# Feed-forward GEMMs of a decoder trunk in groups of two column blocks, six of sixteen k tiles by seven block products instead of eight

## The chip, the cores and the metric

One NeuronCore of a Trainium2 chip runs the whole program in one launch. The metric is the device time of that launch in microseconds. The other engines beside TensorE (PE) are VectorE (DVE), ScalarE (ACT), GpSimd (POOL) and SyncE (SP), which issues nearly all DMAs.

## The reference, cut to what matters

A two-layer decoder trunk on 256 tokens of width 2048, all in float32. Each layer is attention, an output projection, and a SwiGLU feed-forward of inner width 5632; layer a has sparse attention, layer b dilated attention, and both also attend to 256 memory tokens. What the change rewrites is the feed-forward:

```python
def swiglu(h, w_gate, w_up, w_down):
    return (jax.nn.silu(h @ w_gate) * (h @ w_up)) @ w_down
...
    h = h + o
    return h + swiglu(rms_norm(h, norm_ffn), w_gate, w_up, w_down)
```

`w_gate` and `w_up` are 2048 x 5632, `w_down` is 5632 x 2048. The output is the last `h` after a final RMSNorm.

## The kernel before

Float32 accuracy comes from splitting. Every operand is written as hi + lo (two numbers of PE's float32r type): `split` lets ACT copy the source into `hi` (L56) and DVE subtract it, giving `lo` (L57); with a gain the lines are L59 and L60. One product of a 128 x 128 tile of x (stationary) by a 128 x 512 tile of weights (moving) is `mm3`, three matmuls: hi by hi (L64), and the two mixed ones (L65, L66).

A GEMM makes 256 tokens by 512 columns: two PSUM banks (one per token half `tt`), k in 128-row tiles. `load_w` brings weights by DMA in chunks of two k tiles (128 x 1024, 512 KB) into `raw` (four buffers), then splits the chunk into `whi` and `wlo` (three buffers each). `Gemm.run` then issues four `mm3` per chunk. The pools `wp` and `mm_ps` are opened once at the top and live through the whole program; the transposition tiles `aux` have three, later four PSUM banks.

In the feed-forward (`ffn`) each of 11 blocks of 512 columns does a gate GEMM, Silu on ACT (L744), an up GEMM, and a product on DVE (L750) that gives the tile `hb`. Four PE transposes per token half (`heads_T`, L231) turn `hb` into k tiles for the down GEMM, evicted from `aux` by ACT (`hThi`) and DVE (`hTlo`). The transposes are deferred: `at(..., 2, 4)` lists them as side steps, and `Side.tick` runs one after so many `mm3` of the next GEMM. The blocks are done in two halves, six and five, each followed by four down GEMMs of 24 or 20 k tiles whose sums are added to the residual `h`.

What sets the order: PE runs strictly in the order in which the program is written. The other queues (DVE, ACT, SP, POOL) are put in order by a scheduler at build time, and each then runs in that fixed order, waiting by semaphores.

Before the first FFN stands `project_out("a_w_out", ...)`, between the layers a GEMM on `w_kv_shared`, and before the second FFN `project_out("b_w_out", ...)`.

Of the kernel before, what the change touches and what calls it, by code (L numbers as in the profile page):

```python
# [8 lines left out]
F32 = mybir.dt.float32  # L9
# [7 lines left out]
P = 128  # L17
# [8 lines left out]
NFA = 6  # L26
# [5 lines left out]
CK = 2  # L32
# [3 lines left out]
def decoder_trunk(ctx: ExitStack, tc: tile.TileContext, a: dict, out: bass.AP):  # L36
# [3 lines left out]
    wp = ctx.enter_context(tc.tile_pool(name="wp", bufs=4))  # L40
    xp = ctx.enter_context(tc.tile_pool(name="xp", bufs=4))
# [66 lines left out]
    class Gemm:  # L108
        def __init__(self, chunks, xs, ncols, nk, gain=None):
            self.chunks, self.xs, self.ncols, self.nk, self.gain = chunks, xs, ncols, nk, gain  # L110
            self.k = 0
            self.ps = [mm_tile() for _ in range(2)]
# [47 lines left out]
    cs = const.tile([P, 2, 2, HD], F32, name="cs")  # L160
    gains = const.tile([P, 7, KT], F32, name="gains")
    mask_a = const.tile([P, 2 * P], BF16, name="mask_a")
    mask_c = const.tile([P, 2, NCMP], BF16, name="mask_c")
    peT = const.tile([P, 2, 32], F32, name="peT")
    gbias = const.tile([P, 36], F32, name="gbias")
    w2 = const.tile([P, 2, 2, HD], F32, name="w2")
    h = const.tile([P, 2, D], F32, name="h")
    const.tile([P, 80], F32, name="padc")
# [38 lines left out]
    def new_xs():  # L207
        ts = [pair(lambda i: xp.tile([P, 4, T], F32R, tag=("xhi", "xlo")[i], name=("xhi", "xlo")[i]))
              for _ in range(4)]
        xs = [(t[0][:, i, :], t[1][:, i, :]) for t in ts for i in range(4)]  # L210
        return ts, xs

    def residual_block(ps, nb, ssq, ts, gain=None):
# [4 lines left out]
        deferred.extend(at([lambda k2=k2: to_xT(nb, k2, ts, gain) for k2 in range(2)], 3, 5))  # L218

    def to_xT(nb, k2, ts, gain):  # L220
        srcs = [h[:, tt, (nb * 4 + k2 * 2 + i) * P:(nb * 4 + k2 * 2 + i + 1) * P]
                for i in range(2) for tt in range(2)]
        dst = tuple(t[:, k2 * 2:k2 * 2 + 2, :].rearrange("p c t -> p (c t)") for t in ts[nb])
# [13 lines left out]
    def scaled_tables(r, scale, tag):  # L237
        t = small.tile([P, 2, 2, HD], F32, tag=tag, name=tag, bufs=1)
# [123 lines left out]
    def load_memT(c):  # L362
        if c > 0:
# [4 lines left out]
            memT.extend((t[0][:, i, :], t[1][:, i, :]) for i in range(2))  # L368
# [4 lines left out]
    def load_first(i):  # L373
# [4 lines left out]
        memT.append((first_t[0][:, i, :], first_t[1][:, i, :]))  # L378
# [62 lines left out]
    mem_v(ps, mv_b)  # L441
    tab_k = scaled_tables(x_r, 1.0, "tabk")
# [4 lines left out]
    KTt = [pair(lambda i: pa.tile([P, 2, 272], F32R, name=f"KT{g}{i}")) for g in range(2)]  # L447
    V = [pair(lambda i: pa.tile([P, 2, 256], F32R, name=f"V{b}{i}")) for b in range(2)]
# [252 lines left out]
    def project_out(name, nk, ready, gi):  # L701
        ts, xs = new_xs()
        ssq = new_ssq()
        gain = lambda k: gains[:, gi, k:k + 1]
# [8 lines left out]
        for i in range(2):  # L713
# [3 lines left out]
            residual_block(g[i].ps, i, ssq, ts, gain)  # L717
        for nb in range(2, 4):
            ps = gemm(ob[nb], osx, 512, nk)
            residual_block(ps, nb, ssq, ts, gain)  # L720
        return xs, finish_rstd(ssq, 4)

    xs, f_r = project_out("a_w_out", KT, 6, 2)
    sub.close()
    stack.close()

    def ffn(pre, xs, f_r, fp, down_last):
        gb = wblocks(pre + "_w_gate", NFB, KT // CK)
        ub = wblocks(pre + "_w_up", NFB, KT // CK)

        def half(b0, b1):
            hs = []

            def to_hT(hb):
                t = pair(lambda i: fp.tile([P, 4, T], F32R, tag=("hThi", "hTlo")[i], name=("hThi", "hTlo")[i], bufs=7))
                hs.extend((t[0][:, i, :], t[1][:, i, :]) for i in range(4))
                return heads_T(hb, t)

            for b in range(b0, b1):
                ps = gemm(gb[b], xs, 512, KT)  # L740
                sg = []
                for tt in range(2):
                    s = fp.tile([P, 512], F32, tag="sg", name="sg", bufs=2)
                    nc.scalar.activation(s, ps[tt], AF.Silu, scale=f_r[:, tt:tt + 1])  # L744
                    sg.append(s)
                ps = gemm(ub[b], xs, 512, KT)
                hb = []
                for tt in range(2):
                    t = work.tile([P, 512], F32, tag="hb", name="hb", bufs=4)
                    nc.vector.scalar_tensor_tensor(t, ps[tt], f_r[:, tt:tt + 1], sg[tt], op0=ALU.mult, op1=ALU.mult)  # L750
                    hb.append(t)
                deferred.extend(at(to_hT(hb), 2, 4))
            return hs

        hs = half(0, NFA)
        w = a[pre + "_w_down0"]
        for nb in range(4):
            ps = gemm([w[nb, c] for c in range(4 * NFA // CK)], hs, 512, 4 * NFA)
            for tt in range(2):
                hbk = h[:, tt, nb * 512:(nb + 1) * 512]  # L760
                nc.vector.tensor_add(hbk, ps[tt], hbk)
        hs = half(NFA, NFB)
        w = a[pre + "_w_down1"]
        n = 4 * (NFB - NFA)
        down_last([[w[nb, c] for c in range(n // CK)] for nb in range(4)], hs, n)

    with tc.tile_pool(name="fa", bufs=1) as fp:
        def down_last(db, hs, n):
            global_ssq = new_ssq()
            ts, nxt = new_xs()  # L770
            for nb in range(4):
                ps = gemm(db[nb], hs, 512, n)
                residual_block(ps, nb, global_ssq, ts)
# [242 lines left out]
```

## Time and profile before

| | |
|---|---|
| three timed runs | 2092.44, 2093.40, 2094.06 us (median 2093.4) |
| the profiled execution | 2094.15 us, its span 2092.4 us |
| PE busy | 2077.3 us, 99% of the span, 9687 matmuls in the records |
| DVE, ACT busy | 1203.0 us (57%), 1009.5 us (48%) |
| first matmul of feed-forward a | 417.28 us |
| the two stretches shown below | 438.5 to 1127 us in feed-forward a, 1372.6 to 2072 us in feed-forward b |
| DMA | 396 MB, 189 GB/s over the span |

A PE row's duration includes the pipeline's fill and drain, so the pace of PE is the distance between the starts of matmuls, not their duration. The same holds a little for DVE and ACT: of two instructions that stand back to back the second starts some 0.08 us before the first has ended.

### The profile page before, as it was taken

Reading aid. Unit: us, or ns where it says so; the run is one execution under the profiler, and the core shown is the slowest. Engines: PE = TensorE matmul, PEld = TensorE weight load, DVE = VectorE, ACT = ScalarE, POOL = GpSimd, SP = SyncE. Lnnn points to the kernel's source line nnn. Section 1 sums busy time; section 2 is a strip of 40 time slices with the busy share of each in tenths; the row PEclk is TensorE's granted clock in tenths of the full one; section 3 lists DMA queues with packets and bytes.
Section 4 is the critical chain, followed back from the end, with each engine's and each line's share of the span. In section 5 each row is a group of like instructions: output and inputs, shape, how many; then the busy total and the mean of one; then the engine's idle time right before and its main releaser. Section 6 shows DMA issues by size and latency. Waiting matters only on the chain.

```text
span 2092.4 us, 25692 instructions
## 1 busy us (share of the span) xinstructions
PE 2077.3 (99%) x9687; PEld 1726.9 (83%) x9687; DVE 1203.0 (57%) x1727; ACT 1009.5 (48%) x1384; POOL 7.0 (0%) x26
## 2 busy tenths in 40 slices
PE   9999999999999999999999999999999999999998
PEld 7898888888888888888888888888888888888886
DVE  6767897554444554445555678754445544445454
ACT  7655565544444433444444555644444434444443
POOL 0000000000000000000000000000000000000000
PEclk9999999999999999999999999999999999999999
DMA  8757634555555566555555654555555566655564
GB/s 302 240 183 242 210 101 142 183 189 191 190 188 189 189 194 195 190 188 190 188 191 184 196 168 142 183 190 188 189 190 190 190 193 193 189 191 190 189 193 152
DMA packets 112013, 396.31 MB, mean 189 GB/s; under 512 B 12944, under 2 KB 13328, under 8 KB 111504
## 3 DMA queue, kind: packets, MB, share of 16 engines
q1 hardware_dynamic: 111600, 393.61, 57.9%
q8 instruction: 76, 1.25, 0.3%
q10 hardware_dynamic: 288, 1.05, 0.1%
q14 instruction: 49, 0.40, 0.1%
HBM read 392.51 MB, written 2.10 MB: 189 GB/s over the span
## 4 chain that ended last, share of the span: by engine, by line
PE 97%; DVE 2%; ACT 1%; issue 0%; DMA 0%; SPq 0%; POOLq 0%; POOL 0%; DVEq 0%; ACTq 0%
PE mm L64 31%; PE mm L66 30%; PE mm L65 30%; PE aux L231 1%; PE aux L199 1%; PE aux L66 1%; PE aux L65 1%; PE aux L64 1%; DVE wlo L57 0%; PE cmp L514 0%; PE cmp L513 0%; DVE E L269 0%; DMA memT_raw<-in_memT_dram 0%; DVE E L641 0%; ACT whi L56 0%
## 5 line engine op out<-in xcount | busy, mean ns | idle before, releaser
L57 DVE TENSOR_TENSOR wlo<-raw,whi 128x1024 fp32r<-128x1024 f32 (+1 forms) x656 | 795.3, 1213 | 781.2 <-ACT whi L56 776.0
L56 ACT ACTIVATE whi<-raw 128x1024 fp32r<-128x1024 f32 (+1 forms) x656 | 690.6, 1053 | 891.9 <-PE mm L65 871.2
L64 PE MATMUL mm<-whi,xhi 128*128 128x512 f32 (+1 forms) x1856 | 724.6, 390 | 0.0
L66 PE MATMUL mm<-wlo,xhi 128*128 128x512 f32 (+1 forms) x1856 | 716.9, 386 | 0.0
L65 PE MATMUL mm<-whi,xlo 128*128 128x512 f32 (+1 forms) x1856 | 716.2, 386 | 0.0
L66 PEld LDWEIGHTS mm<-wlo,xhi 128*128 128x128 f32 x1856 | 348.4, 188 | 71.8
L65 PEld LDWEIGHTS mm<-whi,xlo 128*128 128x128 f32 x1856 | 348.9, 188 | 65.7
L64 PEld LDWEIGHTS mm<-whi,xhi 128*128 128x128 f32 x1856 | 348.6, 188 | 65.8
L64 PE MATMUL mm<-whi,hThi 128*128 128x512 f32 x704 | 275.2, 391 | 0.0
L66 PE MATMUL mm<-wlo,hThi 128*128 128x512 f32 x704 | 274.0, 389 | 0.0
L65 PE MATMUL mm<-whi,hTlo 128*128 128x512 f32 x704 | 273.9, 389 | 0.0
L66 PEld LDWEIGHTS mm<-wlo,hThi 128*128 128x128 f32 x704 | 132.1, 188 | 27.8
L65 PEld LDWEIGHTS mm<-whi,hTlo 128*128 128x128 f32 x704 | 132.2, 188 | 27.2
L64 PEld LDWEIGHTS mm<-whi,hThi 128*128 128x128 f32 x704 | 132.2, 188 | 26.8
L60 DVE SCALAR_TENSOR_TENSOR wlo<-raw,gains,whi 128x512 fp32r<-128x512 f32 x160 | 113.9, 748 | 46.4 <-ACT whi L59 46.1
L59 ACT ACTIVATE whi<-raw,gains 128x512 fp32r<-128x512 f32 x160 | 108.0, 718 | 60.9 <-PE mm L65 54.1
L64 PE MATMUL mm<-whi,ohi 128*128 128x512 f32 x256 | 102.1, 399 | 2.2 <-ACT whi L59 2.2
L66 PE MATMUL mm<-wlo,ohi 128*128 128x512 f32 x256 | 100.4, 392 | 0.1
L65 PE MATMUL mm<-whi,olo 128*128 128x512 f32 x256 | 100.2, 391 | 0.0
L64 PEld LDWEIGHTS mm<-whi,ohi 128*128 128x128 f32 x256 | 48.5, 189 | 12.3 <-ACT whi L59 3.2
L66 PEld LDWEIGHTS mm<-wlo,ohi 128*128 128x128 f32 x256 | 48.3, 189 | 11.0 <-DVE wlo L60 0.8
L65 PEld LDWEIGHTS mm<-whi,olo 128*128 128x128 f32 x256 | 48.6, 190 | 9.3
(235 smaller groups left out, 1104.7 us busy)
## 6 DMA issues: line engine op xcount, KB each, us to landing
raw<-in_a_w_gate_dram SPq DMA_DIRECT2D x88, 512.0 KB, 4.3
raw<-in_a_w_up_dram SPq DMA_DIRECT2D x88, 512.0 KB, 3.7
raw<-in_a_w_down_dram SPq DMA_DIRECT2D x88, 512.0 KB, 3.8
raw<-in_b_w_gate_dram SPq DMA_DIRECT2D x88, 512.0 KB, 4.1
raw<-in_b_w_up_dram SPq DMA_DIRECT2D x88, 512.0 KB, 3.8
raw<-in_b_w_down_dram SPq DMA_DIRECT2D x88, 512.0 KB, 4.3
raw<-in_a_w_out_dram SPq DMA_DIRECT2D x32, 512.0 KB, 3.8
raw<-in_b_w_in_dram SPq DMA_DIRECT2D x32, 512.0 KB, 4.1
```

The source lines that it names most:

```text
L56: nc.scalar.activation(hi, src, AF.Copy)
L57: nc.vector.tensor_sub(lo, src, hi.bitcast(F32))
L59: nc.scalar.activation(hi, src, AF.Copy, scale=gain)
L60: nc.vector.scalar_tensor_tensor(lo, src, gain, hi.bitcast(F32), op0=ALU.mult, op1=ALU.subtract)
L64: nc.tensor.matmul(o, l[0], r[0], start=start, stop=False)
L65: nc.tensor.matmul(o, l[1], r[0], start=False, stop=False)
L66: nc.tensor.matmul(o, l[0], r[1], start=False, stop=stop)
L199: nc.tensor.transpose(ps[:, i * P:(i + 1) * P], s, ident)
L231: nc.tensor.transpose(ps[:, i * P:(i + 1) * P], tok[tt][:, i * P:(i + 1) * P], ident)
```

## The change

The 11 gate and 11 up blocks become 11 groups: group b holds gate block b and up block b, so that a step works on two column blocks by two token halves, four banks `b1` to `b4`. For six of the sixteen k tiles of a group (three pairs, `NPR` = 3) the 2 x 2 block product (two k tiles by two token halves on the left, two k tiles by two column blocks on the right) is made by seven products of sums of blocks (Strassen's scheme) and not eight. The other ten k tiles are "plain" steps of four `mm3`. Group 0 of a layer is all plain (16 steps). The down GEMMs become groups too: the inner width is now done in three portions of 4, 4 and 3 blocks, and each portion has two down groups of 1024 columns over 16, 16 or 12 k tiles; the last portion of layer b keeps plain GEMMs. In all 30 groups have the seven products.

The sums on the token side are made once for each operand (`Paired.finish`, four extra 128-column tiles per pair) and split with it. Those on the weight side are made by DVE on 128 x 1536 "quarters" that a DMA of 768 KB brings (`q11`, `q12`, `q22`, `q21`), and each of the seven operands is split by ACT and DVE (`qhi`, `qlo`, two buffers). Some products serve two banks: ACT copies a bank (`keep`), DVE adds to or subtracts from banks and makes `rest`. `run_groups` interleaves the plain steps of a group with the seven products of the next, by a table (`spacing`).

Room is made for this: `whi`/`wlo` have two buffers in the FFN and not three, `aux` has one PSUM bank there and not four, and the pools are opened and closed by phase (attention a, FFN a, attention b, FFN b); the memory keys and values of layer b are written to DRAM early and read back.

The core of the diff (rewritten layout helpers, constants moved between pools and tables left out):

```diff
-NFA = 6
+PORTIONS = ((0, 4), (4, 8), (8, 11))
+NPR = 3
+NSL = 8
+QW = NPR * 512
...
-    wp = ctx.enter_context(tc.tile_pool(name="wp", bufs=4))
-    mm_ps = ctx.enter_context(tc.tile_pool(name="mm_ps", bufs=4, space=PSUM))
+    def open_phase(name, raws, parts, mms, auxs):
+        nonlocal wp, wbufs, mm_ps, mm_tags, aux_ps
+        wp = phase.enter_context(tc.tile_pool(name="w" + name, bufs=1))
+        wbufs = raws, parts
+        mm_ps = phase.enter_context(tc.tile_pool(name="m" + name, bufs=1, space=PSUM))
+        mm_tags = mms
+        phase.enter_context(aux_stack)
+        aux_ps = aux_stack.enter_context(tc.tile_pool(name="x" + name, bufs=auxs, space=PSUM))
+    ATT = (("mm", 4), ("mm", 4))
+    FFN = (("b1", 2), ("b2", 2), ("b3", 2), ("b4", 1))
...
+        def finish(self, q, f):
+            n = 4
+            if self.sums:
+                n = NSL
+                nc.vector.tensor_sub(f[:, 4, :], f[:, 0, :], f[:, 3, :])
+                nc.vector.tensor_sub(f[:, 6, :], f[:, 1, :], f[:, 0, :])
+                nc.vector.tensor_sub(f[:, 5, :], f[:, 4, :], f[:, 1, :])
+                nc.vector.tensor_add(f[:, 7, :], f[:, 2, :], f[:, 5, :])
+            split(self.S[0][:, q, :n, :], self.S[1][:, q, :n, :], f[:, :n, :])
...
+        def product(self, b, s, t, side, start=False):
+            hl = [fq.tile([P, QW], F32R, tag=n, name=n, bufs=2) for n in ("qhi", "qlo")]
+            split(hl[0], hl[1], t)
+            for q in range(NPR):
+                mm3(self.bank[b], self.op.slot(q, s), tuple(v[:, q * 512:(q + 1) * 512] for v in hl),
+                    start and q == 0, q == NPR - 1, True)
+                side.tick()
...
+            def s1():
+                self.q12 = self.load(1)
+                nc.vector.tensor_add(self.q11, self.q11, self.q12)
+                self.new(2)
+                self.product(2, 4, self.q11, side, True)
+                self.p5 = self.keep(2)
+            def s2():
+                self.q22 = self.load(2)
+                nc.vector.tensor_add(self.q11, self.q11, self.q22)
+                b2 = self.new(1)
+                self.product(1, 5, self.q11, side, True)
+                nc.vector.tensor_add(b2, b2, self.p1)
+                u2 = self.keep(1)
+                nc.vector.tensor_sub(self.bank[2], self.bank[2], u2)
+            def s3():
+                nc.vector.tensor_add(self.q12, self.q12, self.q22)
+                self.product(1, 6, self.q12, side)
+                self.r = fq.tile([P, 512], F32, tag="rest", name="rest", bufs=2)
+                nc.vector.tensor_sub(self.r, self.p5, self.bank[1])
...
+        def plain(self, c, side):
+            if c == 0:
+                self.new(3)
+            ws = load_w(self.rest[c], 512)
+            last = c == len(self.rest) - 1
+            k = self.k0 + c
+            for b in ((3, 0, 1, 2) if last else (0, 1, 2, 3)):
+                x = self.op.xs[k](b % 2)
+                mm3(self.bank[b], x, ws[b // 2], c == 0 and (b == 3 or self.k0 == 0), last, True)
+                side.tick()
+
+    def spacing(n):
+        base = {16: (3, 2, 2, 2, 2, 2, 2), 10: (2, 1, 1, 2, 1, 2, 1), 6: (1, 1, 1, 1, 0, 1, 1)}[n]
+        return base, n - sum(base)
...
-                deferred.extend(at(to_hT(hb), 2, 4))
+                deferred.extend(at(hop().heads(j, hb), 5, 8))
...
+    def open_ffn(name):
+        nonlocal fh, fq, fpool
+        fbufs[0] = 2
+        open_phase(name, 4, 2, FFN, 1)
...
+    phase.close()
+    open_phase("b", 4, 3, ATT, 4)
...
+    for i in range(4):
+        nc.gpsimd.dma_start(mb[i], memkv[i])
```

Two places in the queues, as the built programs have them.

SP where the output projection of layer a gives way to the FFN, before (names carry buffer numbers; in brackets the semaphores that a row waits for):

```order
L76 DMA raw_4360<-in_a_w_out_dram 128x1024 [waits DMAHW4_49,DVE_49]
L76 DMA raw_4378<-in_a_w_out_dram 128x1024 [waits DMAHW5_49,DVE_49]
L76 DMA raw_4396<-in_a_w_out_dram 128x1024 [waits DMAHW6_49,DVE_49]
L76 DMA raw_4432<-in_a_w_gate_dram 128x1024 [waits DMAHW7_49,DVE_49]
L76 DMA raw_4459<-in_a_w_gate_dram 128x1024 [waits DMAHW0_49,DVE_49]
L76 DMA raw_4486<-in_a_w_gate_dram 128x1024 [waits DMAHW1_49,DVE_49]
L76 DMA raw_4504<-in_a_w_gate_dram 128x1024 [waits DMAHW2_49,DVE_49]
```

The same place of SP now (`gu_0` holds the first gate and up blocks, `gu_q` the quarters):

```order
L98 DMA raw_4370<-in_a_w_out_dram 128x1024 [waits DMAHW0_49,DVE_49]
L98 DMA raw_4388<-in_a_w_out_dram 128x1024 [waits DMAHW1_49,DVE_49]
L98 DMA raw_4406<-in_a_w_out_dram 128x1024 [waits DMAHW2_49,DVE_49]
L98 DMA raw_4461<-in_a_gu_0_dram 128x1024 [waits DMAHW4_49,DMAHW5_49,DMAHW3_49,DMAHW6_49,DVE_49,PE_49]
L98 DMA raw_4488<-in_a_gu_0_dram 128x1024
L98 DMA raw_4515<-in_a_gu_0_dram 128x1024
L860 DMA q11_4533<-in_a_gu_q_dram 128x1536 [waits Pool_49]
L98 DMA raw_4551<-in_a_gu_0_dram 128x1024
L98 DMA raw_4569<-in_a_gu_0_dram 128x1024 [waits DMAHW7_49,DVE_49]
```

The first weights of the FFN waited for DVE's last read of one `raw` buffer; they now wait for PE too, and the count of that semaphore is the one which the last matmul of the output projection brings. The first weights of phase b and of FFN b wait in the same way.

DVE after a gate/up block, where the two token halves of `hb` are transposed (`hTlo<-aux` empties a transposition tile), before:

```order
L57 TENSOR_TENSOR wlo_6367<-raw_6364,whi_6366 128x1024
L750 SCALAR_TENSOR_TENSOR hb_6324<-mm_6178,rstd_4423,sg_6174 128x512
L750 SCALAR_TENSOR_TENSOR hb_6326<-mm_6179,rstd_4423,sg_6176 128x512
L57 TENSOR_TENSOR wlo_6385<-raw_6382,whi_6384 128x1024
L57 TENSOR_TENSOR hTlo_6329<-aux_6344,hThi_6328 128x4x128
L57 TENSOR_TENSOR wlo_6403<-raw_6400,whi_6402 128x1024
L57 TENSOR_TENSOR hTlo_6329<-aux_6357,hThi_6328 128x4x128
```

The same place of DVE now, after the fourth group of layer a:

```order
L78 TENSOR_TENSOR qlo_5924<-q11_5920,qhi_5923 128x1536
L983 SCALAR_TENSOR_TENSOR hb_5850<-mm_5322,rstd_4433,hb_5850 128x512
L983 SCALAR_TENSOR_TENSOR hb_5853<-rest_5427,rstd_4433,hb_5853 128x512
L78 TENSOR_TENSOR wlo_5891<-raw_5888,whi_5890 128x1024
L885 TENSOR_TENSOR q11_5920<-q11_5920,q12_5956 128x1536
L900 TENSOR_TENSOR q12_5956<-q12_5956,q22_5993 128x1536
L78 TENSOR_TENSOR wlo_5941<-raw_5938,whi_5940 128x1024
L78 TENSOR_TENSOR qlo_5961<-q11_5920,qhi_5960 128x1536
L78 TENSOR_TENSOR hTlo_4877<-aux_5897,hThi_4876 128x4x128
L78 TENSOR_TENSOR wlo_5978<-raw_5975,whi_5977 128x1024
L892 TENSOR_TENSOR q11_5920<-q11_5920,q22_5993 128x1536
L78 TENSOR_TENSOR hTlo_4877<-aux_5913,hThi_4876 128x4x128
```

One `wlo` stood between the second `hb` and the emptying of the first tile; now two `wlo`, two additions of quarters and a `qlo` stand there. With one `aux` bank PE's second four transposes (`aux_5913`) wait for that `hTlo`.

## Rows read from the trace of the kernel before

**Rows 1.** The page: busy time, share of span, instructions of each engine.

```profile
PE 2077.3 (99%) x9687; PEld 1726.9 (83%) x9687; DVE 1203.0 (57%) x1727; ACT 1009.5 (48%) x1384; POOL 7.0 (0%) x26
```

**Rows 2.** The page: chain that ended last, by engine.

```profile
PE 97%; DVE 2%; ACT 1%; issue 0%; DMA 0%; SPq 0%; POOLq 0%; POOL 0%; DVEq 0%; ACTq 0%
```

**Rows 3.** Windows over both feed-forwards: length, busy us per engine, clock, DMA, GB/s.

```profile
438.50:1127.00 688.50, 688.50 (x3093) 570.09 (x3092) 346.77 (x313) 297.91 (x311) 0.00 (x0) 1.00 0.59 190
1372.60:2072.00 699.40, 699.40 (x3129) 579.12 (x3128) 353.14 (x321) 299.99 (x310) 0.00 (x0) 1.00 0.59 190
```

**Rows 4.** Timeline of a gate GEMM: start, duration, engine, line, op, tiles.

```profile
599.38 1.23 DVE L57 TENSOR_TENSOR wlo<-raw,whi 128x1024 fp32r<-128x1024 f32 x1 [0.93 <-ACT whi L56]
...
600.53 0.68 DVE L57 TENSOR_TENSOR hTlo<-aux,hThi 128x512 fp32r<-128x512 f32 x1
...
601.53 0.39 PE L64 MATMUL mm<-whi,xhi 128*128 128x512 f32 x1
...
604.22 1.06 ACT L56 ACTIVATE whi<-raw 128x1024 fp32r<-128x1024 f32 x1 [1.66 <-PE mm L65]
...
604.25 0.39 PE L64 MATMUL mm<-whi,xhi 128*128 128x512 f32 x1
```

**Rows 5.** Groups by line and shape: count, busy us, mean ns, idle before.

```profile
L57 DVE TENSOR_TENSOR wlo<-raw,whi 128x1024 fp32r<-128x1024 f32 x640 | 783.7, 1225 | 769.5 <-ACT whi L56 764.4 <-PE cmp L514 2.0
...
L56 ACT ACTIVATE whi<-raw 128x1024 fp32r<-128x1024 f32 x640 | 680.0, 1063 | 877.8 <-PE mm L65 858.2 <-issue 8.0 <-PE cmp L513 3.4
...
L750 DVE SCALAR_TENSOR_TENSOR hb<-mm,rstd,sg 128x512 f32<-128x512 f32 x44 | 32.2, 748 | 0.0
L57 DVE TENSOR_TENSOR hTlo<-aux,hThi 128x512 fp32r<-128x512 f32 x44 | 30.3, 688 | 7.4 <-ACT hThi L56 7.4
...
L56 ACT ACTIVATE hThi<-aux 128x512 fp32r<-128x512 f32 x44 | 26.0, 590 | 21.1 <-PE aux L231 21.1
...
L60 DVE SCALAR_TENSOR_TENSOR xlo<-aux,gains,xhi 128x256 fp32r<-128x256 f32 x32 | 14.6, 480 | 4.2 <-ACT xhi L59 4.1
L59 ACT ACTIVATE xhi<-aux,gains 128x256 fp32r<-128x256 f32 x32 | 14.3, 466 | 1.8 <-PE aux L199 1.8
...
L57 DVE TENSOR_TENSOR wlo<-raw,whi 128x548 fp32r<-128x548 f32 x16 | 11.6, 726 | 11.7 <-ACT whi L56 11.7
...
L56 ACT ACTIVATE whi<-raw 128x548 fp32r<-128x548 f32 x16 | 10.6, 664 | 14.1 <-PE mm L65 13.1 <-PE mm L66 1.0
...
L641 DVE TENSOR_SCALAR E<-E,coef 128x128 f32<-128x128 f32 x24 | 6.7, 281 | 0.0
```

**Rows 6.** Timeline where one token half is transposed.

```profile
640.97 0.60 PE L231 MATMUL aux<-ident,hb 128*128 128x128 f32 x4
...
641.33 0.48 PE L64 MATMUL mm<-whi,xhi 128*128 128x512 f32 x1
...
641.61 0.60 ACT L56 ACTIVATE hThi<-aux 128x512 fp32r<-128x512 f32 x1 [0.96 <-PE aux L231]
```

**Rows 7.** Timeline where the output projection of layer a ends and FFN a begins.

```profile
403.29 13.93 SPq L76 DMA_DIRECT2D raw<-in_a_w_gate_dram  x6
...
417.06 0.39 PE L66 MATMUL mm<-wlo,ohi 128*128 128x512 f32 x1
417.28 0.39 PE L64 MATMUL mm<-whi,xhi 128*128 128x512 f32 x1
```

**Rows 8.** DMA issues: KB each, median us to landing.

```profile
raw<-in_a_w_gate_dram SPq DMA_DIRECT2D x88, 512.0 KB, 4.3
raw<-in_a_w_up_dram SPq DMA_DIRECT2D x88, 512.0 KB, 3.7
...
mask_b<-in_mask_b_dram SPq DMA_DIRECT2D x1, 384.0 KB, 5.3
```

**Rows 9.** Windows at the program's start.

```profile
8.00:12.00 4.00, 3.54 (x9) 2.76 (x10) 3.13 (x6) 3.16 (x6) 0.00 (x0) 0.57 0.96 351
12.00:16.00 4.00, 4.00 (x19) 3.27 (x18) 3.05 (x5) 2.90 (x6) 0.00 (x0) 1.00 0.98 359
```

More of the change, by code (lines that the diff above doesn't have):

```diff
@@ L205, in transposed, with new_x, __init__, turn @@
                       ps[:, i * T:(i + 1) * T], gain(i))
[L207 to L213, printed above, removed]
+    def new_x():
+        return pair(lambda i: xp.tile([P, XW], F32R, tag=("xhi", "xlo")[i], name=("xhi", "xlo")[i]))
+    class Plain:
+        def __init__(self, gain=None):
+            x = new_x()
+            self.gain = gain
+            self.ts = [tuple(v[:, i * 1024:(i + 1) * 1024].rearrange("p (k t) -> p k t", t=T) for v in x) for i in range(4)]
+            self.kt = [tuple(v[:, i, :] for v in t) for t in self.ts for i in range(4)]
+            self.xs = [cols(pr) for pr in self.kt]
+        def turn(self, nb, k2):
+            to_xT(nb, k2, self.ts, self.gain)
@@ L725, in decoder_trunk @@
     stack.close()
[L727 to L746, printed above, removed]
+    phase.close()
@@ new lines, in spacing, with run_groups @@
+    def spacing(n):
+        base = {16: (3, 2, 2, 2, 2, 2, 2), 10: (2, 1, 1, 2, 1, 2, 1), 6: (1, 1, 1, 1, 0, 1, 1)}[n]
+        return base, n - sum(base)
+    def run_groups(groups):
+        for i, g in enumerate(groups):
+            side = take()
+            n = len(g.rest)
+            nxt = groups[i + 1] if i + 1 < len(groups) else None
+            c = 0
+            if nxt is not None and nxt.q is not None:
+                base, left = spacing(n)
+                for p, s in enumerate(nxt.steps(side)):
+                    for _ in range(base[p] + (left if p == 6 else 0)):
+                        g.plain(c, side)
+                        c += 1
+                    if c == n and g.done is not None:
+                        side.flush()
+                        g.done(g)
+                        g.done = None
+                    s()
+            while c < n:
+                g.plain(c, side)
+                c += 1
+            side.flush()
+            if g.done is not None:
+                g.done(g)
@@ new lines, in ffn, with hop, gate_up @@
+    def ffn(pre, op, f_r, last):
+        gq, gs = a[pre + "_gu_q"], a[pre + "_gu_s"]
+        groups = []
+        for pi, (b0, b1) in enumerate(PORTIONS):
+            final = pi == len(PORTIONS) - 1
+            nk = 4 * (b1 - b0)
+            hp = {}
+            def hop(pi=pi, nk=nk, final=final, hp=hp):
+                if "op" not in hp:
+                    x = pair(lambda i: fh.tile([P, XW], F32R, tag=("hThi", "hTlo")[i], name=("hThi", "hTlo")[i]))
+                    hp["op"] = Paired(x, nk, sums=not (final and pre == "b"))
+                return hp["op"]
+            def gate_up(g, j, hop=hop):
+                up = g.bank[3]
+                if g.r is not None:
+                    nc.vector.tensor_add(g.r, g.r, g.bank[3])
+                    up = g.r
@@ L753, in half @@
[L753 to L765, printed above, removed]
@@ L898, in final @@
         side = take()
-        g.run(0, nch - 3, side)
-        ws = [load_w(db[3][c], 512) for c in range(nch - 3, nch)]
+        g.run(0, nch - 2, side)
+        ws = [load_w(db[3][c], 512) for c in range(nch - 2, nch)]
         k0 = g.k
```

294 lines of the change are left out of this document (231 added, 63 removed).

## The prediction

> **What bounds the kernel now.** I read the busy times first. PE is busy for 99% of the span [rows 1], and the chain of work that ended last is PE for 97% [rows 2], so time is PE time. But a busy PE is not yet a PE at its peak, so I went to the stretches and to single starts. In both feed-forwards PE is busy for the whole window at a granted clock of 1.00, with DVE at half (346.77 of 688.5 us) and DMA at 0.59 [rows 3]. In the timeline the same matmul of a chunk starts at 601.53 and at 604.25 [rows 4]; twelve matmuls lie between, so one costs 2.72 / 12 = 0.2267 us and an `mm3` 0.68 us. The reader should see there that ACT waited 1.66 us for PE to release a buffer: ACT and DVE follow PE and do not hold it up. And at the change from projection to FFN there is no gap: 417.06, then 417.28, because the first gate weights were asked for at 403.29 [rows 7].
>
> **What it removes.** 30 groups save one product in eight over three pairs, 3 `mm3` or 9 matmuls each. That is 270 matmuls (8178 instead of 8448 with 512 columns in the built programs), and 270 x 0.2267 = 61.2 us. Nothing else leaves PE; the transposes stay as many. This holds only while PE stays the bound, so everything else is about what makes it wait.
>
> The Trainium skill ("TensorE: Matmul & The Clock Gate", section "Wait — 56ns, not 53.3ns?") has a warm 512-column matmul start every 215.7 ns. The trace's step is 226.7 ns [rows 4], and the measurement decides; by the page the gain would be 58.2 us and the sum 3 us later.
>
> **What it adds beside PE.** A group of 61 `mm3` takes PE 61 x 0.68 + 0.72 (eight transposes, 0.36 for four [rows 6]) = 42.2 us. DVE's cost by width [rows 5]: 726 ns at 548 and 1225 at 1024 give 1.05 ns per column, so 1.76 us at 1536; ACT likewise 664 and 1063 give 1.49 us. Per group DVE has 10 plain splits (12.25), 7 product splits (12.3), 4 additions of quarters (7.0), 4 bank updates at 0.69 (2.8), two `hb` at 0.75 (1.5) and 1.4 to 4.7 us for the transposed heads: 37 to 40.5 us, less 0.08 us for each back-to-back start (the first two of [rows 4]), some 30 of them: 35 to 38. So DVE goes from half to some 87% and stays below PE on average. A DVE instruction that writes PSUM isn't in this trace; I take 0.69 as for the ones that read it, with 0.28 (128 columns [rows 5]) and 1.2 as ends. ACT gets some 26 us. DMA bytes are nearly the same.
>
> **Term 1, the single transposition bank.** The average hides the order. I walk one group, time 0 at its first plain step. PE: step 1 to 2.72, the first `mm3` of step 2 to 3.40, transposes A to 3.76, three `mm3` to 5.80; there transposes B should start. They need A's bank empty. ACT's order is the `whi` of step 3 (its buffer is freed by step 1 at 2.72, so to 3.8), the `qhi` of the second product (1.49, to 5.2), then A's `hThi` (0.59, to 5.8). DVE in the order shown above does the two additions of quarters and the `wlo` meanwhile, then the `qlo` that can start at 5.2 and ends at 7.0, then A's `hTlo`, to 7.65. PE waits from 5.80 to 7.65, 1.9 us. Before, one `wlo` stood there and three further banks were free. This falls on 9 groups (the third and fourth of their portions). The second groups put half of the tile through another path: `hTlo` of 256 columns, 0.42 by slope, 1.6 us, 5 groups. In the first groups ACT alone empties the bank (0.2 us), but eight small sums at 0.28 and two 1024-wide splits push the `qlo` of the third product 1.0 us past PE: 1.2 us, 5 groups. Sum 17.1 + 8.0 + 6.0 = 31 us. Ends: 0, if DVE runs so far ahead that it meets A earlier, and 60, if the delay is passed on to a second wait in each group. The down groups have no transposes; there the tightest place in the same walk, the third product, keeps 1 us of slack.
>
> **Term 2, the three phase starts.** The first weights of FFN a, of phase b and of FFN b wait for the last matmul of the phase before. So the 13.8 us of lead [rows 7] becomes nothing. A 512 KB load lands 3.7 to 4.3 us after its issue [rows 8], I take 4.0; the ACT split takes 1.06, so PE starts again after 5.1 us. After two matmuls it waits for `wlo`: 1.23 - 0.45 = 0.8. In the FFN starts two tiles of x are still to be transposed through the one bank, and ACT's queue has the `qhi` of the first quarter between the two halves of the first tile. That quarter is the fourth load in line: 2.36 MB at 355 GB/s [rows 9] is 6.6 us, with the 2.5 us that a 4.0 us load spends beside its 1.5 us of transfer 9.1. Then 1.49 + 1.76 for its split and 0.48 for the other half of the tile [rows 5]: 12.8. PE would be there at 5.1 + 0.8 + 2.72 + 0.36 + 0.68 = 9.7, so 3.1 more. And the clock: at the program's start, where PE had been waiting for loads, the granted clock was 0.57 between 8 and 12 us and 9 matmuls started instead of 19 [rows 9]; I take 1.5 us for that after each gap. 5.1 + 0.8 + 3.1 + 1.5 = 10.5, twice 21. At the start of phase b, two tables (0.64 MB) stand ahead on SP and 2 MB of memory keys are read beside them on POOL's queue: at half of 355 GB/s the first weights land at 6.6 + 2.5 = 9 us, alone at 5.8; I take 8, and 2.4 as before for split, `wlo` and clock: 10. Sum 31 us; ends 15 (three times 5.1) and 42.
>
> The Trainium skill ("DMA: Bandwidth & Descriptors", section "Anatomy of one DMA — SWDGE (gpsimd) path") fits 2.0 us plus bytes over 436 GB/s, 3.2 us for 512 KB; the trace shows 3.7 to 4.3 [rows 8]. By it the starts would cost 2.4 us less.
>
> **Term 3, the last portion of layer a.** It has only three gate/up groups, so the third pair's token sums are made in the iteration whose first product reads them: transposes B end at 8.0, copy, sums and a 1024-wide split end near 12, PE wants them at 9.6: 2.5 us. The iteration with six plain steps gives PE 45 `mm3` (30.6 us) and DVE 31 us of work that also waits: 3 us. And four tiles of the next x pass the one bank in the last six steps, each waiting for 0.59 + 0.69 of the one before: 4.5 us. Sum 10; ends 3 and 16.
>
> The early DRAM copy of the memory keys (2 MB) falls where DMA has room and nothing waits for it soon: nothing. The end of the program has the same chain after the last matmul: nothing.
>
> **Sum.** The profiled execution took 2094.15 us (its span 2092.4 and 1.75 around it): 2094.15 - 61.2 + 31 + 31 + 10 = 2105. The median of the runs is 0.75 us below this execution: 2104 us, 0.5% slower. The gain is the sure term; three groups of waits of about its size stand against it.
>
> **Rivals.** (1) *The queues keep ahead.* DVE averages 87%, and between its waits for PE's buffers it has some 5 us per group free; if the `hTlo` of term 1 finds its turn while PE is still in step 2, only the phase starts (15) and the DVE-bound iteration (3) stay: 2094.15 - 61.2 + 18 = 2051. For it: the slack. Against it: the order is fixed, and the `qlo` ahead waits for an ACT split that itself waits for PE. This is the case on the other side of my forecast. (2) *DVE becomes the bound.* It decides once DVE's work per group passes 42.2 us, so 0.13 to 0.2 us more for each of some 35 instructions, as additions that write PSUM or waits between ACT and DVE might bring. At 45 us per group in place of term 1: 30 x 2.8 = 84, and 2094.15 - 61.2 + 84 + 41 = 2158. Against it: both kinds of addition have close rows. (3) That the change doesn't do what it says is excluded by the count of matmuls.
>
> **How the numbers follow.** Forecast 0.64, rival 1 0.25, rival 2 0.11. The forecast's own range is 2084 to 2126 (terms 1 and 2 each off by some 10). This kernel's runs can tell about 0.2%, 4.2 us. Faster by more than that: all of rival 1 and 0.08 of the forecast, 0.33. Within: 0.13 of the forecast. Slower: its other 0.43 and rival 2, 0.54. The range goes from near rival 1 to halfway to rival 2: 2058 to 2136.
>
> **What would show it.** In the changed profile: matmuls 270 fewer and still 0.227 us apart inside a step; PE idle before the second `aux<-ident,hb` of a group, released by DVE's `hTlo`, near 1.9 us; three gaps of PE of 5 us or more, each ended by a load and its split, with a granted clock below 1.00 after them; DVE near 85% in the FFN windows. I am wrong if PE is busy without gaps through the FFN windows (rival 1), or if PE waits mostly for `qlo` and `wlo` in the down groups too (rival 2).

## The result, and the profile after

The changed kernel takes 2107.0 us (median of four runs, 2106.5 to 2108.4) against 2093.2 us (four runs on the same chip): 1.0067 times as long, 95% interval 1.0049 to 1.0084. Slower, and 3 us above the forecast of 2104. The profiled execution has a span of 2104.7 us, 12.3 more than before.

The page's busy times and its chain of waits, which answer to [rows 1] and [rows 2]:

```profile
PE 2033.8 (97%) x9417; PEld 1680.9 (80%) x9417; DVE 1644.3 (78%) x2097; ACT 1190.3 (57%) x1552; POOL 9.6 (0%) x30
PE 84%; DVE 9%; issue 3%; DMA 2%; ACT 2%; SPq 0%; DVEq 0%; POOLq 0%; POOL 0%; ACTq 0%
```

270 matmuls are gone. PE is busy 43.5 us less, yet the span is longer: PE now stands still. The chain that was PE for 97% has DVE, DMA and ACT in it. What PE waits for (engine, line, tile; the tile and engine waited for; us in total, times, longest):

```profile
PE aux L305 <- DVE hTlo L78: 23.6, 14, 1.8
PE mm L86 <- ACT whi L80: 11.0, 3, 9.3
PE mm L86 <- ACT whi L77: 9.8, 2, 4.9
PE aux L227 <- DVE xlo L81: 5.4, 2, 2.8
PE aux L227 <- DVE xlo L78: 2.8, 2, 1.4
PE mm L86 <- ACT hThi L77: 1.5, 1, 1.5
...
PE mm L88 <- DVE qlo L78: 1.2, 3, 0.4
PE mm L87 <- DVE hTlo L78: 1.2, 1, 1.2
...
PE mm L88 <- DVE wlo L78: 1.1, 4, 0.4
```

The first row is the transposition bank. The second (9.3 of its 11.0 us) and the third are the three phase starts, the fourth is the bank of x behind the FFN starts.

*One group* (PE, ACT and DVE, timeline; start, duration, idle before and releaser in brackets):

```profile
577.09 0.60 PE L305 MATMUL aux<-ident,hb 128*128 128x128 f32 x4
...
579.37 0.40 PE L88 MATMUL mm<-wlo,xhi 128*128 128x512 f32 x1
581.55 0.66 PE L305 MATMUL aux<-ident,hb 128*128 128x128 f32 x4 [1.78 <-DVE hTlo L78]
...
577.34 1.47 ACT L77 ACTIVATE qhi<-q 128x1536 fp32r<-128x1536 f32 x1
578.72 0.58 ACT L77 ACTIVATE hThi<-aux 128x512 fp32r<-128x512 f32 x1
...
576.33 1.76 DVE L900 TENSOR_TENSOR q<-q,q 128x1536 f32<-128x1536 f32 x1
578.01 1.22 DVE L78 TENSOR_TENSOR wlo<-raw,whi 128x1024 fp32r<-128x1024 f32 x1
579.14 1.75 DVE L78 TENSOR_TENSOR qlo<-q,qhi 128x1536 fp32r<-128x1536 f32 x1
580.81 0.68 DVE L78 TENSOR_TENSOR hTlo<-aux,hThi 128x512 fp32r<-128x512 f32 x1
```

The second four transposes could start at 579.60. ACT's copy is done at 579.30, but DVE first does a sum of quarters, `wlo` and `qlo`; `hTlo` ends at 581.49, and PE starts at 581.55. The distance from 579.37 is 2.18 us where 0.23 would do: 1.95 us lost.

*The start of FFN a*, which answers to [rows 7] (PE, then ACT and DVE):

```profile
415.25 0.39 PE L88 MATMUL mm<-wlo,ohi 128*128 128x512 f32 x1
420.53 0.79 PE L86 MATMUL mm<-whi,xhi 128*128 128x512 f32 x1 [4.89 <-ACT whi L77]
...
422.38 0.63 PE L86 MATMUL mm<-whi,xhi 128*128 128x512 f32 x1
422.81 0.63 PE L87 MATMUL mm<-whi,xlo 128*128 128x512 f32 x1
...
430.22 1.09 PE L227 MATMUL aux<-ident,h 128*128 128x128 f32 x4 [2.56 <-DVE xlo L81]
...
426.04 0.47 ACT L80 ACTIVATE xhi<-aux,gains 128x256 fp32r<-128x256 f32 x1 [2.81 <-PE aux L227]
426.41 1.48 ACT L77 ACTIVATE qhi<-q 128x1536 fp32r<-128x1536 f32 x1
427.79 0.46 ACT L80 ACTIVATE xhi<-aux,gains 128x256 fp32r<-128x256 f32 x1
...
427.92 1.76 DVE L78 TENSOR_TENSOR qlo<-q,qhi 128x1536 fp32r<-128x1536 f32 x1 [0.89 <-ACT qhi L77]
429.59 0.48 DVE L81 SCALAR_TENSOR_TENSOR xlo<-aux,gains,xhi 128x256 fp32r<-128x256 f32 x1
```

Two stops: 4.89 us for the first load and its split, then 2.56 us for the bank of x, whose second half stands behind `qhi` on ACT and `qlo` on DVE. After the first stop matmuls start 0.43 us apart and not 0.23; the windows (us, then busy time of PE, PEld, DVE, ACT, POOL, granted clock, DMA share, GB/s) show a granted clock near the lower of its two levels (1.2 of 2.4 GHz) and, later, the upper one:

```profile
423.00:427.00 4.00, 4.00 (x14) 3.22 (x13) 1.68 (x2) 1.19 (x3) 0.00 (x0) 0.57 1.02 407
440.00:450.00 10.00, 10.00 (x46) 8.29 (x45) 8.62 (x6) 6.33 (x6) 0.00 (x0) 1.00 0.55 194
```

*The whole account.* I take the distance between successive starts on PE, less 0.2267 us for each 512-column matmul [rows 4] and 0.09 for each transpose, and call what is left lost. From the end of the projection of layer a (414 us) to the end it is 11.5 us before and 86.1 us after, 74.6 more. 74.6 - 61.2 = 13.4, against 12.3 more in the span: the account closes to 1 us. Below "lost" means this.

### The profile page after: what moved, and what is told of

It is laid out like the page before. It is cut to its first block, busy times and chain, and to the rows that moved or that the text cites. A ratio compares the mean times of both kernels' runs of the same rounds, so it can differ in the third digit from the quotient of the medians.

```text
span 2104.7 us, 25507 instructions
## 1 busy us (share of the span) xinstructions
PE 2033.8 (97%) x9417; PEld 1680.9 (80%) x9417; DVE 1644.3 (78%) x2097; ACT 1190.3 (57%) x1552; POOL 9.6 (0%) x30
## 4 chain that ended last, share of the span: by engine, by line
PE 84%; DVE 9%; issue 3%; DMA 2%; ACT 2%; SPq 0%; DVEq 0%; POOLq 0%; POOL 0%; ACTq 0%
PE mm L86 26%; PE mm L87 26%; PE mm L88 26%; DVE wlo L78 3%; DVE qlo L78 2%; DVE q L885 1%; PE aux L227 1%; ACT qhi L77 1%; PE aux L305 1%; PE aux L88 1%; PE aux L87 1%; PE aux L86 1%; ACT whi L77 1%; DVE hTlo L78 1%; DVE hb L983 1%
## 5 line engine op out<-in xcount | busy, mean ns | idle before, releaser
L77 ACT ACTIVATE whi<-raw 128x1024 fp32r<-128x1024 f32 (+1 forms) x476 | 498.0, 1047 | 522.0 <-PE mm L87 451.2
L78 DVE TENSOR_TENSOR wlo<-raw,whi 128x1024 fp32r<-128x1024 f32 (+1 forms) x476 | 573.4, 1206 | 214.5 <-ACT whi L77 212.8
L86 PE MATMUL mm<-whi,xhi 128*128 128x512 f32 (+1 forms) x1376 | 540.1, 393 | 19.1 <-ACT whi L77 9.8
L88 PE MATMUL mm<-wlo,xhi 128*128 128x512 f32 (+1 forms) x1376 | 533.8, 388 | 0.8 <-DVE wlo L78 0.7
L87 PE MATMUL mm<-whi,xlo 128*128 128x512 f32 (+1 forms) x1376 | 533.0, 387 | 0.0
L78 DVE TENSOR_TENSOR qlo<-q,qhi 128x1536 fp32r<-128x1536 f32 x210 | 368.5, 1757 | 97.2 <-ACT qhi L77 95.5
L77 ACT ACTIVATE qhi<-q 128x1536 fp32r<-128x1536 f32 x210 | 311.8, 1485 | 135.5 <-PE mm L87 128.2
L86 PEld LDWEIGHTS mm<-whi,xhi 128*128 128x128 f32 x1376 | 260.7, 189 | 68.3 <-ACT whi L77 10.6
L88 PE MATMUL mm<-qlo,xhi 128*128 128x512 f32 x420 | 163.9, 390 | 1.2 <-DVE qlo L78 1.2
L86 PE MATMUL mm<-qhi,xhi 128*128 128x512 f32 x420 | 164.3, 391 | 0.0
L87 PE MATMUL mm<-qhi,xlo 128*128 128x512 f32 x420 | 163.5, 389 | 0.0
L86 PEld LDWEIGHTS mm<-whi,hThi 128*128 128x128 f32 x464 | 87.1, 188 | 17.7
```

The costliest lines, as they stand in the source:

```text
L77: nc.scalar.activation(hi, src, AF.Copy)
L78: nc.vector.tensor_sub(lo, src, hi.bitcast(F32))
L86: nc.tensor.matmul(o, l[0], r[0], start=start, stop=False, skip_group_check=more)
L87: nc.tensor.matmul(o, l[1], r[0], start=False, stop=False, skip_group_check=more)
L88: nc.tensor.matmul(o, l[0], r[1], start=False, stop=stop, skip_group_check=more)
```

## The experiments

All times are medians; each ratio is to the kernel before, run on the same chip. The changed kernel is called "the change".

### The second four transposes later (e1)

```diff
-                deferred.extend(at(hop().heads(j, hb), 5, 8))
+                deferred.extend(at(hop().heads(j, hb), 5, 8 if final else 12))
```

> Edit: in the first two portions of both feed-forwards the second four transposes of a group come four ticks later (12 instead of 8), so after the first product and one more mm3; the last portions stay as they are. Theory (term 1: PE stands still only because the second four meet a bank that DVE's hTlo has not emptied): hTlo ends some 1.9 us after the old place and the new one is 2.7 us after it, so 12 of the 14 waits go, 8 of 1.95 us and 4 of 1.68 us, 22 us: 2107 - 22 = 2085 us (2080 to 2092), and nothing else grows by more than a few us. Rival (DVE's work per group is the bound and the wait is only where it shows): the 1.7 us come back before a later qlo or wlo of the same group, 2103 to 2109 us.

Measured: 2083.9 us, 0.995 (0.9936 to 0.9964). PE's waits for the bank, and a stretch of 200 us of the groups:

```profile
PE aux L305 <- DVE hTlo L78: 3.3, 2, 1.8
...
500.00:700.00 200.00, 200.00 (x895) 165.49 (x895) 170.54 (x153) 116.34 (x112) 0.00 (x0) 1.00 0.63 203
```

12 of 14 waits are gone, 23 us came back, and PE is busy in all of the 200 us with DVE at 85%. The work of DVE is the same, so the rival, that its sum is the bound, falls: the wait was a matter of when PE comes to the bank.

### The raw buffers kept over the phases (e2)

```diff
+    wraw = ctx.enter_context(tc.tile_pool(name="wraw", bufs=1))
...
-        raw = wp.tile([P, 1024], F32, tag="raw", name="raw", bufs=wbufs[0])
+        raw = wraw.tile([P, 1024], F32, tag="raw", name="raw", bufs=4)
```

> Edit: the four buffers for raw weights stay open over all phases, everything else is opened and closed per phase as before. Theory (term 2: the gaps at the phase starts are the first loads, which wait for the last matmul of the old phase): the first four weight blocks of each phase now land beforehand, and what is left of a start is the ACT split, 1.3 us, and 0.8 us for wlo. At phase b the gap of 9.3 us falls to 1.5 and the half clock behind it goes: 10 us less. At both FFN starts the first gap of 4.9 us falls to 1.3, but ACT's queue has the qhi of the first quarter ahead of the copies of x, that quarter still waits for the end of the old phase, and PE meets the bank of x some 4 to 5 us long: only 4 us less each. Sum 18: 2089 us (2083 to 2095). Rival A (no second wait at the FFN starts): 3.6 and 3 us of clock each there, 2084 or less with x turned without a gap, 2080. Rival B (the loads are not what the starts wait for, but the closing of the other pools): 2105 to 2108.

Measured: 2089.3 us, 0.9979 (0.9971 to 0.9988). PE's waits (lines are one higher than in the change):

```profile
PE aux L306 <- DVE hTlo L79: 23.8, 14, 2.0
PE aux L228 <- DVE xlo L82: 7.2, 2, 3.7
...
PE mm L87 <- ACT whi L78: 2.4, 2, 1.2
PE mm L87 <- ACT whi L81: 2.3, 3, 0.9
```

The loads' waits fall from 9.8 to 2.4 us and from 11.0 to 2.3, and the bank of x takes more, 7.2 in place of 5.4. Counted from the last matmul of the projection, PE comes to that bank 5.9 us sooner at FFN a and finds it empty only 4.9 us sooner, since ACT's `qhi` now waits for the quarter's load:

```profile
420.82 1.49 ACT L78 ACTIVATE qhi<-q 128x1536 fp32r<-128x1536 f32 x1 [1.61 <-DMA q<-in_a_gu_q_dram]
```

Lost at the three starts: 8.7, 2.5 and 8.7 us, against 12.6, 12.6 and 10.4. The saving of 17.7 is within 0.3 us of the theory, but in part by luck: the starts give 15.7 (FFN b 1.7, where 4 was expected), and 1.6 came from a stretch that the edit doesn't touch, where the clock fell in the profile of the change and not in this one (term 3 below). Both rivals fall.

### The saved matmuls put back (e3)

```diff
+            for rep in range(2 if s == 1 else 1):
+                for q in range(NPR):
+                    mm3(self.bank[b], self.op.slot(q, s), tuple(v[:, q * 512:(q + 1) * 512] for v in hl),
+                        start and q == 0, q == NPR - 1, True)
+                    if rep == 0:
+                        side.tick()
```

> Edit: the nine matmuls of the first block product of each of the 30 groups run twice, the second time over the first, from the same split parts; the result is the same, and 270 matmuls are back, as many as the scheme saved. Theory (PE is the bound, and the waits come from the order of the queues and not from DVE's sum of work): 270 x 0.2267 = 61 us more, and the 14 waits for hTlo stay at 20 to 24 us, since they stand ahead of this product: 2168 us (2160 to 2172). Rival (DVE's sum of work per group sets the waits): the 2.04 us more per group give DVE time, the waits of 23.6 us vanish, and it is 2140 to 2150 us.

Measured: 2165.3 us, 1.0338 (1.0324 to 1.0352): 58.3 more than the change.

```profile
PE aux L305 <- DVE hTlo L78: 21.8, 13, 1.8
```

13 of the 14 waits stay though DVE had 2 us more time in each group. The lost time fell from 86.1 to 82.2 us (that one wait, and the three for `qlo`), and 58.3 + 3.9 = 62.2 is what 270 matmuls cost (the runs of e3 spread over 5.7 us). The gain of 61.2 us was there in full and was spent on waits.

### Phase b's other reads held back (e4), and again with the table first (e9)

```diff
-    nc.sync.dma_start(cs, a["cs"])
+    nc.gpsimd.dma_start(cs, a["cs"])
...
-    nc.sync.dma_start(mask_b, a["mask_b"])
-    for i in range(4):
-        nc.gpsimd.dma_start(mb[i], memkv[i])
...
+    nc.vector.tensor_copy(mask_b[:, 0, 0, :2], tok[0][:, :2])
+    nc.gpsimd.dma_start(mask_b, a["mask_b"])
+    for i in range(4):
+        nc.vector.tensor_copy(mb[i][:, :2], tok[0][:, :2])
+        nc.gpsimd.dma_start(mb[i], memkv[i])
```

> Edit: at the start of phase b the read-back of the memory keys (2 MB) and the mask wait for the first projection, and the rotary table goes to POOL's queue, so that only 0.26 MB runs beside the first weights. Theory (of the 9.3 us at phase b about 4.4 are transfers that share the way with the first weight block): the first block lands 4.0 to 4.5 us after its issue, the gap falls to about 5 us, 2107 - 4.3 = 2102.5 us (2100 to 2104.5). Rival (the gap is the load alone or a release that comes late): the gap stays at 9 us, 2106 to 2108.

Measured: 2107.6 us, 1.0063 (1.005 to 1.0076): nothing gained. The time says that the rival holds; the trace says otherwise (PE, then DVE):

```profile
1156.16 0.67 PE L86 MATMUL mm<-whi,xhi 128*128 128x512 f32 x1 [4.53 <-ACT whi L80]
1159.83 0.80 PE L88 MATMUL mm<-wlo,xhi 128*128 128x512 f32 x1 [2.57 <-DVE wlo L81]
...
1157.91 0.61 DVE L349 TENSOR_SCALAR tabk<-cs,rstd 128x256 f32<-128x256 f32 x2 [3.49 <-DMA cs<-in_cs_dram]
...
1159.04 4.05 DVE L81 SCALAR_TENSOR_TENSOR wlo<-raw,gains,whi 128x512 fp32r<-128x512 f32 x6
```

The first wait fell from 9.30 to 4.53 us as expected. But I had moved the rotary table to POOL's queue, where it landed after 5.9 us, and DVE's queue has the table's scaling ahead of the first `wlo`. The edit made a new wait of 2.57 us. With the first pair of lines of the diff undone:

> Edit, on the changed kernel: at phase b the rotary table stays first on SP's queue as it was, and only the mask and the read-back of the memory keys wait for the first projection. Theory (in the run e4_phase_b_reads_late the first weights came 4.8 us sooner, but DVE's next instruction was the scaling of the rotary table, which waited for the table on POOL's queue, and wlo stood behind it): the table lands first, DVE has done its scaling before the first split, PE starts after some 5.3 us and meets no second wait; with 2.5 us of half clock the start costs 8.3 in place of 12.6 us: 2107 - 4.3 = 2102.5 us (2100 to 2104.5). Rival (the memory read-back is not what delays the first weights): 2105 to 2108.

Measured: 2103.1 us, 1.0048 (1.0036 to 1.0061); PE starts once and goes on:

```profile
1158.53 0.80 PE L86 MATMUL mm<-whi,xhi 128*128 128x512 f32 x1 [5.15 <-ACT whi L80]
```

Phase b loses 7.4 us in place of 12.6. The medians of e4 and e9 are 4.5 us apart. Of these the traces put 2.5 at phase b (9.9 us lost in e4), and they are the place of a 256 KB table in a queue; where the rest arose is not shown.

### The first quarter's split behind x (e5), with filling (e6), with raw kept (e7)

```diff
+            if first:
+                nc.scalar.activation(hl[0][:, :1], self.op.xs[KT - 1](1)[0][:, P - 1:].bitcast(F32), AF.Copy)
             split(hl[0], hl[1], t)
...
-        base = {16: (3, 2, 2, 2, 2, 2, 2), 10: (2, 1, 1, 2, 1, 2, 1), 6: (1, 1, 1, 1, 0, 1, 1)}[n]
+        base = {16: (4, 2, 2, 2, 2, 2, 2), 10: (2, 1, 1, 2, 1, 2, 1), 6: (1, 1, 1, 1, 0, 1, 1)}[n]
```

> Edit, on the changed kernel: the ACT split of the first quarter of each feed-forward stands behind the last copy of x (a one-column copy of that x tile into qhi makes it wait), and the first product comes one plain step later. The loads still wait for the end of the old phase. Theory (the second stop at the FFN starts is the bank of x, whose second copy stands behind that qhi; PE loses 2.7 us there and, having stood still, 1.6 us of half clock after it): both go, the first gap of 5.05 us and the half clock behind it (2.7 us) stay, so an FFN start falls from 12.6 and 10.4 us to 8.3: 6 us less, 2101 us (2097 to 2104). Rival (PE would meet the next weight block late in any case, since all loads share the way): a wait for whi or wlo takes the place of the wait for xlo, 2105 to 2108.

Measured: 2105.5 us, 1.0055 (1.0042 to 1.0068). The FFN starts lose 12.4 and 10.6 us, as before the edit: the theory missed. ACT, DVE and PE:

```profile
428.19 0.47 ACT L80 ACTIVATE xhi<-aux,gains 128x256 fp32r<-128x256 f32 x1 [3.02 <-PE aux L227]
429.05 1.06 ACT L77 ACTIVATE whi<-raw 128x1024 fp32r<-128x1024 f32 x1 [0.38 <-PE mm L87]
430.01 0.45 ACT L80 ACTIVATE xhi<-aux,gains 128x256 fp32r<-128x256 f32 x1
...
430.14 1.23 DVE L78 TENSOR_TENSOR wlo<-raw,whi 128x1024 fp32r<-128x1024 f32 x1 [0.95 <-ACT whi L77]
431.28 0.48 DVE L81 SCALAR_TENSOR_TENSOR xlo<-aux,gains,xhi 128x256 fp32r<-128x256 f32 x1
...
431.91 0.63 PE L227 MATMUL aux<-ident,h 128*128 128x128 f32 x4 [1.85 <-DVE xlo L81]
```

With the quarter out of the way the third weight block stands between the halves of the x tile, 1.06 us on ACT and 1.23 on DVE, and in FFN b a wait of 1.04 us for a `wlo` was added. One neighbour took the place of another. e6 adds this to e5:

```diff
+    def fill(x, n):
+        ps = aux_tile()
+        for i in range(n):
+            nc.tensor.matmul(ps, x[:, :P], x, start=True, stop=True)
```

> Edit, on the kernel of the run before it: while PE waits at the three phase starts it runs matmuls on a finished x tile into the empty transposition bank, 21 at each feed-forward and 41 at phase b, 0.227 us each, so about as long as the gaps; nothing reads them. Theory (the half clock after the starts comes from PE's own standstill): the granted clock stays at 1.0 behind the starts, the matmuls there start 0.227 us apart in place of 0.43, and 2.5 us come back at each of the three: 2101 - 7.5 = 2093.5 us (2091 to 2098). Rival (the clock falls there for another reason, or the pace there is that of the loads and splits): the same time as without the filling, 2099 to 2103.

Measured: 2100.4 us, 1.0032 (1.002 to 1.0045). The same four microseconds behind the start of FFN a, in e5 and then in e6:

```profile
423.00:427.00 4.00, 3.96 (x9) 2.57 (x9) 2.12 (x2) 1.06 (x1) 0.00 (x0) 0.50 1.02 414
```

```profile
417.74 4.92 PE L1042 MATMUL aux<-xhi 128*128 128x512 f32 x21
...
423.00:427.00 4.00, 3.47 (x17) 2.56 (x17) 2.30 (x3) 1.67 (x3) 0.00 (x0) 1.00 1.02 417
```

The granted clock is 1.00 with the filling and 0.50 without, with the same loads in flight: PE's own standstill is what the half clock follows. It gives 5.1 us, not 7.5. A PE at full clock comes sooner to a `wlo` that is not ready (3.5 us of such waits, 1.4 without), and in the stretch of term 3 below the clock fell in e6 and not in e5, 1.6 us. The mechanism held, the size did not.

> Edit: the raw pool kept over all phases and the first quarter's split behind x's copies, together. Theory: with raw kept alone the FFN starts still cost 8.7 us each, of which 3.7 are the bank of x and 1 the half clock behind that; with the quarter behind x what is left is 1.36 for the split, 0.7 for wlo and 1.2 for the second half of x behind the third whi, 3.4 with small change: 2089.3 - 10.6 = 2078.7 us (2074 to 2083). Rival (the bank of x waits for the late quarter's traffic or for the third block in any case): 2085 to 2090.

Measured: 2085.8 us, 0.9959 (0.9946 to 0.9973), in the rival's range: e7 keeps the raw pool and has e5's edit, the FFN starts lose 6.4 and 6.3 us, and 2.0 of each are the bank of x behind the third block, as in e5. The granted clock behind that wait is 0.50 at FFN a (426.5 to 429.5 us), which the theory's 3.4 us left out.

### All together (e8), and the x turn later (e10)

> Edit: the raw pool kept, the first quarter's split behind x's copies, and the second four transposes of a group four ticks later in the first two portions. Theory (the three costs stand in different places and add): 2078.7 - 23 = 2055.5 us (2050 to 2061), 1.8% faster than the kernel before. Rival (with PE closer to its peak DVE's work per group sets the pace): part of the 23 us comes back as waits for qlo and wlo, 2063 to 2075.

e8 is e7 with e1's edit. Measured: 2063.5 us, 0.9855 (0.9842 to 0.9869), 22.2 below e7; e1 alone was 23.1 below the change. Outside the starts it loses 26.0 us, e1 25.4, so nothing came back through DVE. The sum missed because e7 had. e10 moves PE's demand and not the queues:

```diff
-        deferred.extend(at([lambda k2=k2: op.turn(nb, k2) for k2 in range(2)], 3, 5))
+        deferred.extend(at([lambda k2=k2: op.turn(nb, k2) for k2 in range(2)], 3, 9 if nb == 3 else 5))
...
-                nc.scalar.activation(hl[0][:, :1], self.op.xs[KT - 1](1)[0][:, P - 1:].bitcast(F32), AF.Copy)
+                nc.scalar.activation(hl[0][:, :1], self.op.xs[KT - 3](1)[0][:, P - 1:].bitcast(F32), AF.Copy)
```

> Edit, on the kernel of e8_all_three: the second of the two last transpositions of x comes four ticks later (9 instead of 5), and the first quarter's split waits only for the first of them. Theory (what is left at the FFN starts is again one bank: the second half of the first x tile leaves it behind the third whi and wlo, 2 us after PE wants it): the bank is empty when PE comes, 2.1 us less at each FFN start, the wait of 1.2 us for a wlo behind the quarter's qlo stays: 2063.5 - 4.2 = 2059.3 us (2056 to 2062). Rival (the 2 us come back as a longer wait for that wlo): 2062 to 2066.

Measured: 2055.0 us, 0.9817 (0.9803 to 0.983): 4 us better than expected. The waits for `wlo` at the FFN starts went too (2.4 us in e8), and the half clock in the stretch of term 3 below cost 1.3 us less than in e8, which is not the edit's doing. The waits for `xlo` at the FFN starts are gone, and they lose 4.4 and 2.8 us. Its busy times:

```profile
PE 2024.7 (99%) x9417; PEld 1676.5 (82%) x9417; DVE 1639.3 (80%) x2097; ACT 1190.3 (58%) x1554; POOL 11.6 (1%) x30
```

This kernel beats both, by 38 us the one before and by 52 the changed one, and every output is computed as in the changed one.

## Why the prediction was right, point by point

- **PE as the bound, the gain of 61.2 us.** Right: e3 gives 62.2, which its spread cannot tell from 61.2.
- **Term 1, the single transposition bank, 31 us.** 27.6 measured: nine third and fourth groups at 1.95 (1.9 forecast), five second groups at 1.68 (1.6), and the first groups 0.56 in three of five where 1.2 in each was forecast. The walk ended within 0.1 us of the measured wait, by nearly the same way: it had `qlo` wait for ACT's `qhi`, and in the group shown `qhi` is done at 578.81 while `qlo` starts at 579.14, behind `wlo`, in a DVE that runs without a pause from 576.33. e1 shows that it is this wait. The mis-sized part is the `qlo` of the first groups, 1.7 us in place of 6. The Trainium skill ("Perfetto Trace Analysis", section "Optimization Strategy") says that the same gap repeating on the engine that should be saturated can mean too little SBUF or PSUM for the next tile. The trace agrees, 14 gaps of 1.5 to 1.8 us; e1 adds that 12 of them close without another bank.
- **Term 2, the three phase starts, 31 us.** 35.6 lost, 34.8 more than before. Load and split: 5.05 us (5.1 forecast). The 0.8 us for `wlo` is not there (0.04 us at FFN a, where PE ran at half clock). Phase b: 12.6 where 10 was forecast; of its gap of 9.3 us e9 shows some 4 to be the reads beside the first weights. The bank of x: 2.7 (3.1), near by luck. The forecast had PE wait for the quarter's load. In the rows shown `qhi` waits for no load: it follows ACT's first copy of x at 426.04, which waited 2.81 us for PE's transposes, and PE came to these late, at half clock. In e2, where PE comes sooner, `qhi` does wait for the load. The clock was under-sized: 1.5 us per start forecast, 2.7 after the first stop and 1.6 after the second measured at FFN a. e6 shows it to come from the standstill. The step as a whole is shown by e2 and e9.
- **Term 3, the last portion of layer a, 10 us.** 8.1 measured: 3.1 for the third pair's sums (2.5), 3.4 for the turns of the next x (4.5), and 1.6 of half clock behind the first of these, which the forecast did not have. PE waited 1.51 and 1.16 us there (ended at 1058.95 and 1060.60), and then the granted clock is 0.57 in the change; in e2 the same two waits left it at 1.00 (the rows below are of the change, then of e2). The 3 us for the iteration with six plain steps are not there: between 1100 and 1130 us DVE is busy 27.4 us of 30, and apart from the bank's 1.95 nothing waits long. No run tried this portion alone.

```profile
1061.00:1065.00 4.00, 4.00 (x12) 3.13 (x11) 1.76 (x1) 1.97 (x2) 0.00 (x0) 0.57 0.00 0
```

```profile
1057.00:1061.00 4.00, 3.35 (x15) 2.78 (x16) 1.89 (x2) 2.04 (x3) 0.00 (x0) 1.00 0.00 0
```

- **Together** the terms gave 72 us of lost time and there were 74.6; some 4 us of it are small waits that I did not list. That the forecast came within 3 us is in part luck, since the terms missed by 2 to 4 us in both directions. The upper end of its range was called halfway to rival 2, which would be 2131 and not 2136; nothing hangs on it.
- **Rival 1** (the queues keep ahead, 2051) did not happen by itself; e10 reaches 2055 once PE asks later and the loads run ahead. **Rival 2** (DVE the bound, 2158): DVE has 78% of the span and 84% of the stretch from 1440 to 1800 us in FFN b, and e1 ran PE without a gap with DVE at 85%.

## What to carry to other kernels

A saving on the busiest engine is kept only where the others reach its next request in time, and an average load of 85% says nothing on that: walk the fixed order of each queue up to the place where PE comes to a shared buffer. When buffers are given up to make room, look for the two things that they did quietly: further banks let the transposes run ahead of their eviction (argued from the order of the queues; no run here gave a bank back), and a pool that stayed open let loads cross a phase boundary (e2). To close a wait, it was surer here to let PE ask later (e1, e10) than to move one instruction out of a queue (e4, e5), where a neighbour took its place.

## What the runs showed of the hardware that I had not expected

- The clock fell to half after short stops too, but not each time. In e10 PE stood still for 1.20 and 0.53 us at the start of FFN a (416.88 and 418.14), and the window behind is at 0.50; in e2 the same two stops left 417 to 421 us at 1.00. Behind the two waits of term 3 it fell in the change and in eight of the ten experiments, and not in e2 and e5. The waits of 1.78 us in the groups of the change left it alone. First e10, then e2, then the change around the group shown above:

```profile
419.00:422.00 3.00, 3.00 (x11) 2.41 (x10) 0.65 (x1) 0.25 (x1) 1.19 (x1) 0.50 0.85 249
```

```profile
417.00:421.00 4.00, 2.78 (x12) 1.99 (x13) 2.92 (x5) 2.38 (x5) 1.75 (x1) 1.00 0.76 253
```

```profile
575.00:585.00 10.00, 8.22 (x40) 6.53 (x40) 9.86 (x8) 5.27 (x7) 0.00 (x0) 1.00 0.45 140
```

- A DVE addition onto a PSUM bank (128 x 512, in place) took 0.69 us, as much as one that reads the bank and writes SBUF (in the change 0.695 and 0.692 us on average, against 0.681 and 0.687).
- A 768 KB load from SP took 5.5 us to land (median of the gate and up quarters in the change). At phase b the first 512 KB went from its issue to ACT's split in 7.5 us (1153.19 to 1160.69) with 2 MB on POOL's queue and 0.64 MB ahead of it on its own, and in 3.7 us (1151.67 to 1155.39) in e4, with a 256 KB table on POOL's queue.
